# The small products of the inverse in a gated-delta layer, emitted in another order

## The chip, the cores and the metric

The kernel runs on one core of a Trainium2 chip. The metric is the device time of one execution in microseconds. The time before is the median of three runs.

## What is computed

A trunk of two layers over 256 tokens of 2048 channels. Each layer normalises its input, projects it with one wide matrix, feeds three mixers (a convolution module, a gated DeltaNet, a dilated attention) and projects their gated outputs back into the residual stream. A last normalisation follows.

The change touches only the DeltaNet's chunk rule, in which each chunk of each head needs the inverse of a unit lower triangular matrix:

```python
kk = jnp.einsum("bhncd,bhnmd->bhncm", k, k)
lower = jnp.where(strict, beta[..., :, None] * kk * decay, 0.0)
T = lax.linalg.triangular_solve(eye + lower, jnp.broadcast_to(eye, lower.shape),
                                left_side=True, lower=True, unit_diagonal=True)
w_v = jnp.einsum("bhncm,bhnmd->bhncd", T, v * beta[..., None])
```

## The kernel before

All weights stream from HBM in chunks of two (at the output projection of the last piece four) 128-row blocks: `load_weights` (L406) brings a chunk into one of four `raw` buffers, ScalarE rounds it to the high part `whi` (L182), VectorE subtracts to get the low part `wlo` (L190), and TensorE runs three products per block (L450), high by high, high by low and low by high, into an `acc` accumulator. There are three buffers for each part. This projection is a stream of matmuls that goes through the whole kernel, job after job in the order of the list `jobs`; everything else on TensorE (transposes at L230, small products at L223 through the helper `mms`) is put between two units of it.

The order on each engine is fixed when the program is built. Each piece of work is a generator that yields operations with an engine and an estimated cost; `Plan.run` takes, again and again, the operation that can start earliest by its own clocks (ties by priority), emits it, and adds its cost to that engine's clock. What one `mms(...)` call holds is one operation of the plan: nothing of another task comes between its products. Its cost is the sum of 4 times the columns over 2.4 per product, at least 53 ns.

The DeltaNet works on two chunks of 128 tokens and six heads, so on twelve 128x128 triangular matrices per layer. `inverse()` (L841 on) inverts them all. Four 32x32 diagonal blocks of each are inverted on VectorE by substitution, 48 blocks side by side, with the blocks carried there and back through DRAM. Then the inverse is put together by products on TensorE. For one pair of 32-row blocks (a, b), X = L[a,b]' T (into `psx`, copied to `Xs`), and the off-diagonal block is minus a product of X with the other diagonal inverse (into `psy`, negated into `PTs`); the first pair's block is needed transposed as well, in `T64`, which takes one further product. Both pairs done, the same step is made at 64 rows, for the six matrices of each chunk in turn (`i` is 0 or 1). In all 60 products of 32x32 and 24 of 64x64 per layer, all in float32, each of which is two matmul instructions with two weight loads.

A product of 32 rows uses a 32x32 part of TensorE's array. Which part follows from its operands: the row part from the SBUF partitions of the inputs (`Lh(hc)[a, b]` lies on partitions `a`, `Xs[b]` on `b`), the column part from the PSUM partitions of the output (`psx[b]`, `psy[a]`, `psy[b]`). This part is called the product's place here. Before the change all products of one `mms` call have the same place.

`psx` and `psy` are two of four PSUM tiles of the pool `MIX`, which transposes and all small products share. The attention's `att_pair` uses two of the pool and alternates, within one `mms` call, products of the two heads of a pair, whose operands lie in rows 0 to 63 and 64 to 127 of the array. `state(i)` waits for the inverse (`gd["inv"]`) and is the first that reads it.

Of the kernel before, what the change touches and what calls it, by code (L numbers as in the profile page):

```python
# [15 lines left out]
ALU = mybir.AluOpType  # L16
# [7 lines left out]
H = 6  # L24
# [5 lines left out]
HC = 2 * H  # L30
# [127 lines left out]
def _free(ap):  # L158
    n = 1
    for s in ap.shape[1:]:  # L160
        n *= s
    return n
# [3 lines left out]
def hybrid_trunk(ctx, tc, x, norm_w, w_in, conv_qkv_w, a_log, dt_bias, gdn_norm_w, conf_dw_w,  # L166
# [22 lines left out]
    def tt(out_, a, b, op):  # L189
        return ("dve", 70 + _free(out_) / 0.96, lambda: nc.vector.tensor_tensor(out_, a, b, op=op))  # L190

    def ts(out_, a, s1, s2, op0, op1=None):
        extra = 60 if not isinstance(s1, (int, float)) else 0

        def emit():
            if op1 is None:
                nc.vector.tensor_scalar(out_, a, s1, None, op0=op0)
            else:
                nc.vector.tensor_scalar(out_, a, s1, s2, op0=op0, op1=op1)
        return ("dve", 70 + _free(out_) / 0.96 + extra, emit)  # L200

    def cpy(out_, in_):
        return ("dve", 70 + _free(out_) / 0.96, lambda: nc.vector.tensor_copy(out_, in_))
# [14 lines left out]
    def mms(*jobs):  # L218

        def emit():  # L220
            for o, a, b, *f in jobs:
                f = f or (True, True)
                nc.tensor.matmul(o, a, b, start=f[0], stop=f[1])  # L223
        cost = sum(max(53.0, 4 * max(_free(j[1]), _free(j[2])) / 2.4) for j in jobs)
        return ("pe", cost, emit)
# [38 lines left out]
    PTs = cp.tile([128, HC, 128], F32, name="PTs")  # L264
    T64 = cp.tile([64, HC, 64], F32, name="T64")
# [285 lines left out]
    def layer(l):  # L551
# [168 lines left out]
        def decay(b):  # L720
# [28 lines left out]
            if gd["nL"] == 4:  # L749
                plan.spawn(inverse(), 11)  # L750
# [90 lines left out]
        def inverse():  # L841

            yield ("set", gd["L"])
            L = [gd["L0"], gd["L1"]]
            dr = dp.tile([HC, 4, 32, 32], F32, name="dr", tag="dr", bufs=2)
            dr2 = dp.tile([HC, 4, 32, 32], F32, name="dr2", tag="dr2", bufs=2)
            b1, b2 = yield ("get", INV, 2)
            N48, P48 = (b[:48].rearrange("p (r c) -> p r c", c=32) for b in (b1, b2))
            b3 = yield ("get", S256)

            def hop(jobs):
                def emit():
                    for o, i_ in jobs:
                        nc.gpsimd.dma_start(o, i_)
                return ("pool", 2500.0 + 1050.0 * len(jobs), emit)
            qs = [slice(b * 32, (b + 1) * 32) for b in range(4)]
            yield hop([(dr[t * H:(t + 1) * H, b].rearrange("h r c -> r h c"), L[t][qs[b], :, qs[b]])
                       for t in range(2) for b in range(4)])
            yield hop([(N48, dr.rearrange("h b r c -> (h b) r c"))])
            nc.gpsimd.memset(P48, 0.0)  # L860
            nc.gpsimd.memset(b2[:48, 0:1024:33], 1.0)
            yield ("pool", 1500.0, lambda: None)
            for j in range(31, 0, -1):
                w = 32 - j
                tmp = b3[:48, :j * w].rearrange("p (r c) -> p r c", c=w)
                yield tt(tmp, N48[:, :j, j:j + 1].to_broadcast([48, j, w]),
                         P48[:, j:j + 1, j:].to_broadcast([48, j, w]), ALU.mult)
                yield tt(P48[:, :j, j:], P48[:, :j, j:], tmp, ALU.subtract)
            yield hop([(dr2.rearrange("h b r c -> (h b) r c"), P48)])
            yield ("put", INV, [b2])  # L870
            yield ("put", S256, [b3])
            Pd, Td = yield ("get", S384, 2)
            yield hop([(PTs[qs[b], :, qs[b]], dr2[:, b].rearrange("h r c -> r h c")) for b in range(4)]
                      + [(Pd[qs[b]].rearrange("p (h c) -> p h c", c=32), dr2[:, b].rearrange("h r c -> r h c"))
                         for b in range(4)])
            yield ("dve", 500.0, lambda: nc.vector.transpose(Td, Pd))
            P3, T3 = (b.rearrange("p (h c) -> p h c", c=32) for b in (Pd, Td))
            for b in range(2):
                yield cpy(T64[qs[b], :, qs[b]], T3[qs[b]])
            Xs = b1[:, :768].rearrange("p (h c) -> p h c", c=64)  # L880

            def h3(ap, c):
                return ap.rearrange("p (h c) -> p h c", c=c)

            def Lh(hc):
                return L[hc // H][:, hc % H]
            psx, psy = yield ("get", MIX, 2)
            prs = [(slice(0, 32), slice(32, 64)), (slice(64, 96), slice(96, 128))]
            for p, (a, b) in enumerate(prs):
                yield mms(*((psx[b, hc * 32:hc * 32 + 32], Lh(hc)[a, b], T3[a, hc, :]) for hc in range(HC)))  # L890
                yield cpy(Xs[b, :, :32], h3(psx[b, :HC * 32], 32))
                yield mms(*((psy[a, hc * 32:hc * 32 + 32], Xs[b, hc, :32], P3[b, hc, :]) for hc in range(HC)))
                if p == 0:
                    yield mms(*((psy[b, hc * 32:hc * 32 + 32], P3[b, hc, :], Xs[b, hc, :32]) for hc in range(HC)))
                    yield ts(T64[b, :, a], h3(psy[b, :HC * 32], 32), -1.0, None, ALU.mult)
                yield ts(PTs[a, :, b], h3(psy[a, :HC * 32], 32), -1.0, None, ALU.mult)
            yield ("put", S384, [Pd, Td])
            a, b = slice(0, 64), slice(64, 128)
            for i in range(2):
                hs = slice(i * H, (i + 1) * H)  # L900
                yield mms(*((psx[b, j * 64:j * 64 + 64], Lh(i * H + j)[a, b], T64[:, i * H + j, :])
                            for j in range(H)))
                yield cpy(Xs[b, hs, :], h3(psx[b, :H * 64], 64))
                yield mms(*((psy[a, j * 64:j * 64 + 64], Xs[b, i * H + j, :], PTs[b, i * H + j, b])
                            for j in range(H)))
                yield ts(PTs[a, hs, b], h3(psy[a, :H * 64], 64), -1.0, None, ALU.mult)
            yield ("put", MIX, [psx, psy])
            yield ("put", INV, [b1])
            yield ("set", gd["inv"])
# [360 lines left out]
```

## Time and profile before

| | |
|---|---|
| median of 3 runs | 1005.6 us (1005.53 to 1006.33) |
| the profiled execution | 1005.26 us |
| its span | 1003.6 us |
| instructions in it | 18681 |
| ScalarE busy | 548.7 us (55%) |
| GpSimd busy | 48.2 us (5%) |
| DMA, mean over the span | 176 GB/s |

The span goes from the first instruction to the last; the profiled execution's own time has 1.7 us around it. PE is TensorE's matmuls, PEld its weight loads, DVE is VectorE, ACT ScalarE, POOL GpSimd. The end of a matmul in the profile is modelled, and matmuls overlap in time, so the duration of a row that merges several is from the first start to the last end. L223 is the line in `mms`, so all small products of the kernel stand under it, and are told apart by their shapes and tile names. `mix<-b,inv` is a product into a tile of the pool `MIX` from a tile named `b` and one named `inv` (`Xs` lies in an `inv` buffer).

### The profile page before, as it was taken

To read this page: it belongs to the slowest core of one execution; us is meant where nothing else is said; L and a number is where in the kernel's file an instruction comes from. 1 tells how busy PE (TensorE), PEld (TensorE's weight loads), DVE (VectorE), ACT (ScalarE), POOL (GpSimd) and SP (SyncE) were. 2 spreads that over 40 slices of the span, in tenths; PEclk is the share of its full clock that TensorE was granted. 3 is DMA by queue.
4 is the path that set the end of the run, shared out by engine and by line. 5 is a ranking of instruction groups with operands and counts; after the bars stand their busy time and mean duration, and the time that the engine had idled before them with its cause. 6 is when DMAs were issued, how large, how long until landed. Compare 5 with 4: busy or idle time off the path is not lost.

```text
span 1003.6 us, 18681 instructions
## 1 busy us (share of the span) xinstructions
PE 990.7 (99%) x7107; PEld 939.6 (94%) x7107; DVE 747.9 (75%) x1491; ACT 548.7 (55%) x1063; POOL 48.2 (5%) x69
## 2 busy tenths in 40 slices
PE   8999999999999999999999999999999999999996
PEld 8999999999999989888899999999999999998886
DVE  6587599998899666655557767999888987666554
ACT  7665345544676674444455633554447777544443
POOL 1000200100010000000000020002000100000000
PEclk9999999999999999999999999999999999999999
DMA  8665566654444635766656655566444456467644
GB/s 272 178 202 170 154 178 179 186 152 133 145 145 144 198 105 171 232 226 218 210 183 180 197 166 170 176 180 190 139 140 133 143 173 201 129 195 221 212 166 158
DMA packets 113365, 176.86 MB, mean 176 GB/s; under 512 B 8314, under 2 KB 80828, under 8 KB 113276
## 3 DMA queue, kind: packets, MB, share of 16 engines
q1 hardware_dynamic: 111660, 172.66, 55.9%
q0 software_dynamic: 1616, 3.02, 1.1%
q8 instruction: 55, 0.90, 0.4%
q14 instruction: 34, 0.28, 0.1%
HBM read 170.67 MB, written 4.98 MB: 175 GB/s over the span
## 4 chain that ended last, share of the span: by engine, by line
PE 96%; DMA 1%; issue 1%; ACT 1%; DVE 0%; SPq 0%; POOLq 0%; POOL 0%; ACTq 0%
PE acc L450 86%; PE mix L223 6%; PE mix L230 3%; DMA b<-in_x 1%; DMA raw<-in_w_out 1%; PE acc L459 0%; PE mix L733 0%; ACT b L182 0%; DVE wlo L190 0%; ACT whi L182 0%; SPq L406 0%; DVE HT L190 0%; ACT HT L182 0%; SPq L389 0%; PE mix L338 0%
## 5 line engine op out<-in xcount | busy, mean ns | idle before, releaser
L182 ACT ACTIVATE whi<-raw 128x768 fp32r<-128x768 f32 (+4 forms) x373 | 336.6, 902 | 390.9 <-PE acc L450 328.7
L190 DVE TENSOR_TENSOR wlo<-raw,whi 128x768 fp32r<-128x768 f32 (+4 forms) x373 | 383.1, 1027 | 204.4 <-ACT whi L182 194.9
L450 PE MATMUL acc<-HT,whi 128*128 128x256 f32 x2304 | 420.8, 283 | 0.0
L450 PEld LDWEIGHTS acc<-HT,whi 128*128 128x128 f32 x2304 | 356.1, 189 | 1.6 <-issue 1.5
L450 PE MATMUL acc<-HT,wlo 128*128 128x256 f32 x1152 | 325.4, 282 | 0.0
L450 PE MATMUL acc<-whi,HT 128*128 128x384 f32 (+1 forms) x1024 | 271.2, 346 | 0.1
L450 PEld LDWEIGHTS acc<-HT,wlo 128*128 128x128 f32 x1152 | 216.0, 188 | 0.0
L450 PEld LDWEIGHTS acc<-whi,HT 128*128 128x128 f32 x1024 | 179.6, 188 | 2.3 <-issue 1.0
L450 PE MATMUL acc<-wlo,HT 128*128 128x384 f32 (+1 forms) x512 | 172.7, 337 | 0.0
L450 PE MATMUL acc<-whi,YT 128*128 128x512 f32 (+1 forms) x512 | 152.8, 382 | 0.0
L450 PEld LDWEIGHTS acc<-whi,YT 128*128 128x128 f32 x512 | 93.9, 188 | 20.2
L187 DVE SCALAR_TENSOR_TENSOR b<-b,dw,b 128x255 f32<-128x255 f32 (+29 forms) x240 | 104.3, 461 | 0.2
L450 PE MATMUL acc<-wlo,YT 128*128 128x512 f32 (+1 forms) x256 | 97.7, 382 | 0.0
L450 PEld LDWEIGHTS acc<-wlo,HT 128*128 128x128 f32 x512 | 96.3, 188 | 0.0
L450 PEld LDWEIGHTS acc<-wlo,YT 128*128 128x128 f32 x256 | 48.2, 188 | 10.3
L230 PE MATMUL mix<-ident,b 128*128 128x128 f32 x312 | 51.1, 276 | 1.8 <-DMA b<-in_x 1.4
L182 ACT ACTIVATE b<-mix 128x256 f32<-128x256 f32 (+3 forms) x95 | 38.5, 421 | 19.0 <-PE mix L223 9.9
L187 DVE SCALAR_TENSOR_TENSOR b<-b,cw,b 128x255 f32<-128x255 f32 (+2 forms) x108 | 48.6, 473 | 0.0
L223 PE MATMUL mix<-b,b 128*128 128x128 f32 (+5 forms) x456 | 47.8, 285 | 0.4 <-ACT b L182 0.4
L223 PEld LDWEIGHTS mix<-b,b 128*128 128x128 f32 (+3 forms) x456 | 38.0, 161 | 7.5 <-issue 2.7
L230 PEld LDWEIGHTS mix<-ident,b 128*128 128x128 f32 x312 | 37.8, 141 | 7.1 <-DMA b<-in_x 2.3
L187 DVE SCALAR_TENSOR_TENSOR b<-b,b 128x256 f32<-128x256 f32 (+3 forms) x62 | 31.3, 510 | 2.7 <-ACT b L182 2.6
(149 smaller groups left out, 647.4 us busy)
## 6 DMA issues: line engine op xcount, KB each, us to landing
raw<-in_w_in SPq DMA_DIRECT2D x240, 384.0 KB, 3.1
raw<-in_w_out SPq DMA_DIRECT2D x60, 512.0 KB, 4.7
raw<-in_w_in SPq DMA_DIRECT2D x48, 512.0 KB, 3.5
raw<-in_w_in SPq DMA_DIRECT2D x15, 396.0 KB, 3.5
b<-in_x SPq DMA_DIRECT2D x12, 256.0 KB, 6.0
raw<-in_conf_pw_w SPq DMA_DIRECT2D x4, 512.0 KB, 3.2
X<-b SPq DMA_DIRECT2D x8, 256.0 KB
raw<-in_w_out SPq DMA_DIRECT2D x8, 256.0 KB
```

Of the source, the lines that this page charges most:

```text
L182: lambda: nc.scalar.activation(out_, in_, func, bias=bias, scale=scale, **kw))
L187: lambda: nc.vector.scalar_tensor_tensor(out_, a, s, b, op0=op0, op1=op1))
L190: return ("dve", 70 + _free(out_) / 0.96, lambda: nc.vector.tensor_tensor(out_, a, b, op=op))
L223: nc.tensor.matmul(o, a, b, start=f[0], stop=f[1])
L230: nc.tensor.transpose(o, a, ident)
L450: nc.tensor.matmul(o, w, m, start=first and i == 0 and not (chan and t % 2), stop=last and i == 2, skip_group_check=chan)
```

## The change

In the 32-row step the first products of both pairs are emitted in one call, alternating from pair to pair; the second products of both pairs and the product for `T64` in one call, in threes. In the 64-row step the first products of the second six matrices alternate with the second products of the first six. The copies and negations are the same, each behind the call that it needs.

```diff
             prs = [(slice(0, 32), slice(32, 64)), (slice(64, 96), slice(96, 128))]
-            for p, (a, b) in enumerate(prs):
-                yield mms(*((psx[b, hc * 32:hc * 32 + 32], Lh(hc)[a, b], T3[a, hc, :]) for hc in range(HC)))
+            yield mms(*((psx[b, hc * 32:hc * 32 + 32], Lh(hc)[a, b], T3[a, hc, :]) for hc in range(HC) for a, b in prs))
+            for a, b in prs:
                 yield cpy(Xs[b, :, :32], h3(psx[b, :HC * 32], 32))
-                yield mms(*((psy[a, hc * 32:hc * 32 + 32], Xs[b, hc, :32], P3[b, hc, :]) for hc in range(HC)))
-                if p == 0:
-                    yield mms(*((psy[b, hc * 32:hc * 32 + 32], P3[b, hc, :], Xs[b, hc, :32]) for hc in range(HC)))
-                    yield ts(T64[b, :, a], h3(psy[b, :HC * 32], 32), -1.0, None, ALU.mult)
+            (a0, b0), (a1, b1_) = prs
+
+            def third(hc):
+                c = slice(hc * 32, hc * 32 + 32)
+                return [(psy[a0, c], Xs[b0, hc, :32], P3[b0, hc, :]), (psy[a1, c], Xs[b1_, hc, :32], P3[b1_, hc, :]),
+                        (psy[b0, c], P3[b0, hc, :], Xs[b0, hc, :32])]
+            yield mms(*(m for hc in range(HC) for m in third(hc)))
+            yield ts(T64[b0, :, a0], h3(psy[b0, :HC * 32], 32), -1.0, None, ALU.mult)
+            for a, b in prs:
                 yield ts(PTs[a, :, b], h3(psy[a, :HC * 32], 32), -1.0, None, ALU.mult)
             yield ("put", S384, [Pd, Td])
             a, b = slice(0, 64), slice(64, 128)
-            for i in range(2):
-                hs = slice(i * H, (i + 1) * H)
-                yield mms(*((psx[b, j * 64:j * 64 + 64], Lh(i * H + j)[a, b], T64[:, i * H + j, :])
-                            for j in range(H)))
-                yield cpy(Xs[b, hs, :], h3(psx[b, :H * 64], 64))
-                yield mms(*((psy[a, j * 64:j * 64 + 64], Xs[b, i * H + j, :], PTs[b, i * H + j, b])
-                            for j in range(H)))
-                yield ts(PTs[a, hs, b], h3(psy[a, :H * 64], 64), -1.0, None, ALU.mult)
+
+            def down(i, j):
+                return (psx[b, j * 64:j * 64 + 64], Lh(i * H + j)[a, b], T64[:, i * H + j, :])
+
+            def up(i, j):
+                return (psy[a, j * 64:j * 64 + 64], Xs[b, i * H + j, :], PTs[b, i * H + j, b])
+            hs = [slice(i * H, (i + 1) * H) for i in range(2)]
+            yield mms(*(down(0, j) for j in range(H)))
+            yield cpy(Xs[b, hs[0], :], h3(psx[b, :H * 64], 64))
+            yield mms(*(m for j in range(H) for m in (down(1, j), up(0, j))))
+            yield cpy(Xs[b, hs[1], :], h3(psx[b, :H * 64], 64))
+            yield ts(PTs[a, hs[0], b], h3(psy[a, :H * 64], 64), -1.0, None, ALU.mult)
+            yield mms(*(up(1, j) for j in range(H)))
+            yield ts(PTs[a, hs[1], b], h3(psy[a, :H * 64], 64), -1.0, None, ALU.mult)
             yield ("put", MIX, [psx, psy])
```

## Rows read from the trace of the kernel before

**Rows 1.** Page, part 1: engine, busy us, share of the span, instructions.
```profile
PE 990.7 (99%) x7107; PEld 939.6 (94%) x7107; DVE 747.9 (75%) x1491; ACT 548.7 (55%) x1063; POOL 48.2 (5%) x69
```
**Rows 2.** Waits of TensorE: who for whom, us in total, times, longest.
```profile
PE mix L308 <- POOL pw_neg L316: 1.6, 1, 1.6
PE mix L230 <- DMA b<-in_x: 1.4, 2, 1.3
...
PE mix L230 <- DVE b L197: 0.4, 1, 0.4
```
**Rows 3.** Timeline, TensorE, layer 0: start us, us, line, operation, how many.
```profile
219.48 0.34 PE L450 MATMUL acc<-wlo,HT 128*128 128x384 f32 x1
...
220.00 0.34 PE L450 MATMUL acc<-wlo,HT 128*128 128x384 f32 x1
220.26 0.94 PE L223 MATMUL mix<-b,b 32*32 32x32 f32 x24
221.13 0.62 PE L450 MATMUL acc<-whi,HT 128*128 128x384 f32 x2
221.59 0.34 PE L450 MATMUL acc<-wlo,HT 128*128 128x384 f32 x1
```
**Rows 4.** The same timeline, a batch of 64-row products.
```profile
226.30 0.34 PE L450 MATMUL acc<-wlo,HT 128*128 128x384 f32 x1
226.57 0.91 PE L223 MATMUL mix<-T,b 64*64 64x64 f32 x12
227.41 0.62 PE L450 MATMUL acc<-whi,HT 128*128 128x384 f32 x2
227.86 0.34 PE L450 MATMUL acc<-wlo,HT 128*128 128x384 f32 x1
```
**Rows 5.** The same timeline, two batches of 32-row products back to back.
```profile
215.24 0.84 PE L223 MATMUL mix<-b,inv 32*32 32x32 f32 x21
215.90 0.21 PE L223 MATMUL mix<-inv,b 32*32 32x32 f32 x1
215.92 0.19 PE L223 MATMUL mix<-b,inv 32*32 32x32 f32 x1
...
215.96 0.19 PE L223 MATMUL mix<-b,inv 32*32 32x32 f32 x1
...
215.99 0.19 PE L223 MATMUL mix<-b,inv 32*32 32x32 f32 x1
216.01 0.82 PE L223 MATMUL mix<-inv,b 32*32 32x32 f32 x21
216.77 0.44 PE L230 MATMUL mix<-ident,b 128*128 128x128 f32 x2
```
**Rows 6.** Timeline, TensorE, layer 1: the first and last of eight batches.
```profile
706.38 0.94 PE L223 MATMUL mix<-b,b 32*32 32x32 f32 x24
...
730.90 0.91 PE L223 MATMUL mix<-PTs,inv 64*64 64x64 f32 x12
```
**Rows 7.** Timeline, start of an attention pair's first products, at three cuts.
```profile
281.02 0.38 PE L223 MATMUL mix<-b,b 64*128 64x128 f32 x2
281.02 0.19 PEld L223 LDWEIGHTS mix<-b,b 64*128 64x128 f32 x2 [0.25 <-issue]
281.02 0.30 PEld L223 LDWEIGHTS mix<-b,b 64*128 64x128 f32 x4 [0.25 <-issue]
```
**Rows 8.** Stretches: us; busy us (x) of PE, PEld, DVE, ACT, POOL; clock, DMA.
```profile
240.00:260.00 20.00, 20.00 (x133) 19.93 (x132) 17.50 (x40) 12.15 (x29) 0.00 (x0) 1.00 0.46 138
...
280.00:300.00 20.00, 20.00 (x133) 17.98 (x133) 19.29 (x61) 16.38 (x44) 4.78 (x2) 1.00 0.54 158
780.00:800.00 20.00, 20.00 (x131) 18.44 (x130) 19.55 (x62) 15.40 (x38) 4.90 (x2) 1.00 0.49 139
```
**Rows 9.** Timeline, layer 1: a low part is made, and first read.
```profile
782.40 0.95 DVE L190 TENSOR_TENSOR wlo<-raw,whi 128x768 fp32r<-128x768 f32 x1
...
785.25 0.34 PE L450 MATMUL acc<-wlo,HT 128*128 128x384 f32 x1
```

## The prediction, made before the changed kernel was built

> **What bounds the kernel now.** Page part 1 first: TensorE counts as busy for 990.7 of the span's 1003.6 us, VectorE for 747.9 [rows 1]. A busy TensorE need not be a limiting one, so next the view of its waits: it lists five, from 1.6 down to 0.4 us, 4.5 us in all, and the two above 1 us are start-up (one waits for x to arrive) [rows 2]. The reader is to see that TensorE almost never waits in the middle of the run: what it executes there, in the order written, is the time. So a microsecond of TensorE's own time saved comes off the end, provided that the other engines can follow.
>
> Then the timeline of TensorE where the inverse's small products run. They are not alone: they lie between units of the projection, whose matmuls of 384 columns follow each other every 0.17 us (three from 219.48 to 220.00, 0.52) [rows 3]. A batch of small products is an interruption of that stream, and I price it as the time by which it delays the stream: start of the last wide matmul before to start of the third after it, less 0.52.
>
> 12 products of 32 rows, which are 24 matmuls (each float32 product is two): 220.00 to 221.59 is 1.59, so the price is 1.07 [rows 3]. The 24 have 0.94 us from the first start to the last end; one lasts 0.19, so their 23 steps take 0.75, 0.0325 each. The rest, 1.07 - 0.75 = 0.32, is going into small shapes and out again, paid per interruption.
>
> 6 products of 64 rows, 12 matmuls: 226.30 to 227.86, price 1.04 [rows 4]; 0.91 less some 0.22 for one is 0.69 for the steps.
>
> The 24 products emitted as two batches back to back, 48 matmuls: 1.53 us from 215.24 to the next operation at 216.77 [rows 5]; its steps are 1.53 - 0.12 = 1.41 (the 0.12 is the step out, as 221.13 stands 0.12 behind the last small start in rows 3), with the 0.32 the price is 1.73.
>
> One layer has three of the first kind, one of the third, four of the second: 3 x 1.07 + 1.73 + 4 x 1.04 = 9.10 us. Layer 1 repeats them: eight interruptions of the same counts, the first and the last of them stand in [rows 6].
>
> **The change part by part.**
>
> No product, copy or DMA is added or lost: 60 products of 32 rows and 24 of 64 per layer (168 matmuls), and nine copies or negations on VectorE, before and after. What changes is order, and eight interruptions become five: 48 matmuls (both pairs' first products, alternating), 72 (second products of both pairs, with those for T64), then 12, 24 (`down` of the second half alternating with `up` of the first) and 12 of 64 rows.
>
> Whether neighbours at different places of the array run side by side decides everything, and the trace shows it twice. In rows 5 the first batch writes PSUM partitions 0 to 31, the second 32 to 63. Where they meet, starts of the second (from 215.90) mix with the last of the first (215.92, 215.96, 215.99): seven starts from 215.90 to 216.01 (two are left out there), 0.018 apart, against 0.0325 within a batch, so each place keeps its own pace beside the other. In the attention the two heads of a pair alternate between row halves of the array as the new order would: two 64x128 weight loads end after 0.19 us together, which is what one takes, two matmuls after 0.38, and four loads after 0.30, one step of 0.11 for two [rows 7]. So I take: each place at its own pace, the batch as long as its longest place, plus 0.01 per further place. The other end is no overlap, 0.0325 per matmul.
>
> The batch of 48 has two places: 24 steps as in rows 3, 1.07 + 0.01 = 1.08. Other end: 1.73.
>
> The batch of 72 has three places, 24 matmuls each; two of the places are exactly those of rows 5. 1.07 + 0.02 = 1.09. Three at once no row shows; bounds from the rows: 0.018 per start gives 72 x 0.018 + 0.32 = 1.62; the third place wholly behind the others 1.07 + 0.75 = 1.82; no overlap 2.66. I take 1.09, nearest to what rows 5 and 6 show of two.
>
> Of the 64-row batches two interruptions of 12 stay, 2 x 1.04; the 24 alternate between two places that share neither rows nor columns: 1.04 + 0.01 = 1.05; the other end is 1.04 + 0.69 = 1.73.
>
> The new sum is 1.08 + 1.09 + 2.08 + 1.05 = 5.30. Saved are 3.80 per layer, 7.6 us over two.
>
> Cost at nothing: the VectorE steps between batches have stream units around them before and after; no batch is needed at once. The inverse ends about two interruptions and their spacing sooner (from 220.26 to 226.57, with one batch between, they are 3.15 us apart [rows 3, 4]), so the state steps behind it can be planned some 6 us earlier. The planner's price of a batch is the sum of its products, unchanged in total, so its clock agrees with the old one outside the inverse, but it will place other work differently behind. Luck there can give back only waits in mid-run, under 1 us [rows 2]; what it can cost is the second rival.
>
> Who is late next: TensorE, 3.8 us earlier after each inverse, meets VectorE, which prepares the weights' low parts. VectorE is busy 17.5 of 20 us behind the inverse, but 19.3 and 19.6 of 20 from 280 and 780 on [rows 8]. The tightest place of mid-run: a low part is ready at 782.40 + 0.95 = 783.35 and first read at 785.25, a lead of 1.9 us [rows 9]. I expect the lead to be the same afterwards: it is set by a fixed number of weight buffers, and free time like the 2.5 us from 240 to 260 [rows 8] lets VectorE catch up 3.8 us in the 40 us before the tight stretch.
>
> A rule speaks against it. The Trainium skill says (TensorE: Matmul & The Clock Gate, section "Wait — 56ns, not 53.3ns?") that starts of matmuls never come closer than about 25 ns however small they are. By it the batches of 48 and 72 would be 1.52 and 2.12, and 4.7 us would be saved instead of 7.6. Rows 5 disagree over seven starts, 0.018 apart; whether that pace holds for 72 no row shows.
>
> **Sum.** The profiled execution took 1005.26 us: 1003.6 of span and 1.7 around it. 1005.26 - 7.6 = 997.7. The median of the runs lies 0.3 above the profiled one, so 998.0.
>
> **The rivals.**
> First, products that leave by one PSUM tile take turns. The batch of 48 sends both row places into psx, the 72 into psy. In rows 5 both series come from the same rows of the array; in rows 7 each half has a PSUM tile of its own. So no row shows two row places writing one tile. If they take turns, the 48 costs 1.73 and the 72 as well (T64's products beside one pair's, the other pair's behind), the 24 keeps its gain: 6.6 per layer, 5.0 saved, 1000.6. The Trainium skill has this as a rule (TensorEngine Tiling (Array Packing), section "Gotcha 1: PSUM Pressure": different row tiles can't access one PSUM bank at the same time). Against: the partitions written differ, as they did in rows 5. Chance 0.14, a pace of starts in the 72 slower than the 0.018 of rows 5 included.
>
> Second, VectorE becomes the bound in the tight stretches. If it does not catch up, TensorE reaches 785 3.8 us early and its lead of 1.9 is gone: it waits 1.9 us, and about as much in layer 0, whose stretch is as full. Left: 7.6 - 3.8 = 3.8, 1001.8. For it 19.3 and 19.6 of 20; against it the free time before. Chance 0.12.
>
> Third, it does not do what it says: the places don't overlap in an alternating batch, and only three interruptions fewer per layer count: 3 x 0.32 = 0.96, less the 0.1 that rows 5 already overlap, 1.7 in all, 1003.9. Against it: rows 7. Chance 0.08.
>
> Fourth, slower: a change of place costs as a change of shape does. Going from the stream into a batch takes 0.26 (220.00 to 220.26) instead of 0.17 [rows 3], 0.09 more. If the two matmuls of a product stay together, the three mixed batches change place 23, 35 and 11 times, 69 a layer: 6.2 us, less the third rival's 0.86, is 5.3 a layer, 10.7 in all, 1016. It decides from 0.012 per change on, where it eats that gain. Against: rows 7 change place at every product and show no such gap. Chance 0.04.
>
> **How the numbers follow.** The forecast has 0.62, its own range 996.5 to 999.6 (the third place wholly behind is 0.73 per layer; luck in the order gives 1 us). The first two rivals end at 1000.6 and 1001.8, so 996.4 to 1001.8 leaves out the other two and a little. About 0.2%, 2.0 us, can be told from no change: the forecast and the first two rivals are faster by more, 0.88, of which I leave 0.02 to a planned order behind the inverse that loses all of it and more: 0.86. Within: the third rival, 0.08. Slower: the fourth and that 0.02, 0.06.
>
> **What would show it.** Right: five interruptions per inverse; the batch of 48 no longer than 0.96 us and that of 72 no longer than 0.98 from first start to last end; starts in the 48 about 0.016 apart, with both places in turn; the mid-run waits of TensorE as before. First rival: the 48 at 1.6 us, the 24 of 64 rows still at 0.92. Second: TensorE waits on wlo near 780 to 790. Third: 0.0325 per matmul everywhere; fourth: more. The forecast is wrong if the batch of 72 is above 1.7 us, or if TensorE's mid-run waits grow by more than 2 us.

## The result, and the profile after

The changed kernel takes 998.4 us (median of 4 runs, 996.6 to 999.5) against 1006.0 for the kernel before (4 runs, 1005.5 to 1007.8): a ratio of 0.992, with a 95% interval of 0.990 to 0.994. The forecast was 998.0. The profiled execution took 996.6 us, with a span of 994.8.

The page's first part (engine, busy us, share of the span, instructions), to be held against [rows 1]:

```profile
PE 982.5 (99%) x7107; PEld 933.6 (94%) x7107; DVE 747.4 (75%) x1494; ACT 548.0 (55%) x1060; POOL 48.0 (5%) x69
```

TensorE has the same 7107 matmuls and is busy for 8.2 us less; the span is 8.7 us shorter (1003.55 to 994.83). So the time went where it was looked for, out of TensorE's own stream. What TensorE waits for (who for whom, us in total, times, longest), to be held against [rows 2]:

```profile
PE mix L308 <- POOL pw_neg L316: 1.6, 1, 1.6
PE mix L230 <- DMA b<-in_x: 1.3, 2, 0.9
PE mix L223 <- DVE PTs L197: 0.6, 1, 0.6
PE acc L459 <- DVE HT L190: 0.4, 1, 0.4
PE mix L223 <- DVE inv L203: 0.2, 1, 0.2
```

The two lines with L223 are new: small products of the inverse now wait for a copy and a negation on VectorE. They are small, and the forecast did not have them.

Now the inverse of layer 0 on TensorE's timeline (start us, us, line, operation, how many). The 48 matmuls in place of two batches like that of [rows 3]:

```profile
211.35 0.34 PE L450 MATMUL acc<-wlo,HT 128*128 128x384 f32 x1
211.62 0.95 PE L223 MATMUL mix<-b,b 32*32 32x32 f32 x48
212.49 0.62 PE L450 MATMUL acc<-whi,HT 128*128 128x384 f32 x2
212.95 0.34 PE L450 MATMUL acc<-wlo,HT 128*128 128x384 f32 x1
```

They last 0.95 us, and the 24 alone lasted 0.94. From the last wide matmul before to the third after it is 212.95 - 211.35 = 1.60, less the 0.52 of the stream: a price of 1.08.

The start and end of the 72, to be held against [rows 5]:

```profile
215.82 0.22 PE L223 MATMUL mix<-b,inv 32*32 32x32 f32 x2
215.83 0.21 PE L223 MATMUL mix<-inv,b 32*32 32x32 f32 x1
215.87 0.20 PE L223 MATMUL mix<-b,inv 32*32 32x32 f32 x2
215.88 0.19 PE L223 MATMUL mix<-inv,b 32*32 32x32 f32 x1
...
216.58 0.19 PE L223 MATMUL mix<-inv,b 32*32 32x32 f32 x1
216.70 0.44 PE L230 MATMUL mix<-ident,b 128*128 128x128 f32 x2
```

From 215.82 to 216.58 is 0.76 us for 71 steps, 0.0107 each. T64's matmuls, `mix<-inv,b`, begin at 215.88 as the second and at 216.58 as the 24th, 22 steps of 0.032: each place keeps about the 0.0325 of [rows 3], and three run beside each other.

The 24 of 64 rows, beginning and end, to be held against [rows 4]:

```profile
223.05 0.34 PE L450 MATMUL acc<-wlo,HT 128*128 128x384 f32 x1
223.32 0.27 PE L223 MATMUL mix<-T,b 64*64 64x64 f32 x1
223.32 0.27 PE L223 MATMUL mix<-PTs,inv 64*64 64x64 f32 x1
...
224.01 0.22 PE L223 MATMUL mix<-PTs,inv 64*64 64x64 f32 x1
224.16 0.62 PE L450 MATMUL acc<-whi,HT 128*128 128x384 f32 x2
224.62 0.34 PE L450 MATMUL acc<-wlo,HT 128*128 128x384 f32 x1
```

Both places start at 223.32 and end together; the price is 224.62 - 223.05 - 0.52 = 1.05.

**Where the time came from.** Both kernels run the same 5856 matmuls of the projection stream (L450) in the same order, so one can count them from the start and compare the time at which the same matmul begins. In the table, the layer stretches begin and end at such matmuls (numbers 1380, 2300, 4300 and 5500 of L450) and hold the inverse and the attention behind it; "between" holds the rest between numbers 120 and the last.

| us | start to no. 120 | layer 0 | layer 1 | between | last L450 to the end |
|---|---|---|---|---|---|
| before | 31.95 | 188.34 | 225.17 | 537.10 | 20.99 |
| after | 31.49 | 183.25 | 222.29 | 537.09 | 20.70 |
| difference | -0.46 | -5.09 | -2.88 | -0.01 | -0.29 |

Expected were -3.80 in each layer. Start and end differ from one execution to the next; in a second profile of the changed kernel (first experiment) they are 32.19 and 21.42, while the three columns between agree to 0.01 us. So the layers can be read to about 0.1 us, and 0.75 us of this profile's 8.7 is start and end.

Layer 0 can be cut once more, at number 1993. Up to there, with the inverse, both kernels have the same matmuls, and the changed one takes 136.52 us instead of 140.32: 3.80 less, the forecast itself. From 1993 to 2300, the end of the attention, where the edit changes nothing, it takes 46.73 instead of 48.02: the other 1.29.

In layer 1, TensorE's timeline around the last two batches (in brackets the idle time ahead, and for whom):

```profile
711.89 0.34 PE L450 MATMUL acc<-wlo,HT 128*128 128x384 f32 x1
712.48 0.27 PE L223 MATMUL mix<-T,b 64*64 64x64 f32 x1 [0.25 <-DVE inv L203]
...
715.44 0.34 PE L450 MATMUL acc<-wlo,HT 128*128 128x384 f32 x1
716.33 0.91 PE L223 MATMUL mix<-PTs,inv 64*64 64x64 f32 x12 [0.55 <-DVE PTs L197]
```

A batch otherwise starts 0.27 after the last wide matmul (211.35 to 211.62). Here it is 0.59 and 0.89: 0.32 and 0.62 late. VectorE's timeline says why:

```profile
710.88 0.95 DVE L190 TENSOR_TENSOR wlo<-raw,whi 128x768 fp32r<-128x768 f32 x1
711.87 0.56 DVE L203 COPY inv<-mix 64x384 f32<-64x384 f32 x1
...
714.62 0.56 DVE L203 COPY inv<-mix 64x384 f32<-64x384 f32 x1
715.21 0.48 DVE L187 SCALAR_TENSOR_TENSOR b<-b,dw,b 128x250 f32<-128x250 f32 x1
715.72 0.55 DVE L197 TENSOR_SCALAR PTs<-mix 64x384 f32<-64x384 f32 x1
```

The copy that the 24 need ends at 712.43, behind a low part of the weights that VectorE took first; the negation that the last 12 wait for, as they write the part of `psy` that it reads, ends at 716.27, behind a copy and another step (L187). From 714.62 on VectorE goes from one instruction to the next; the inverse's next batch is due sooner than its queue gets to it. In layer 0, instead, 1.29 us more than 3.80 came back. The kernel before waits twice at the end of that layer's attention:

```profile
367.90 1.28 PE L230 MATMUL mix<-ident,b 128*128 128x128 f32 x7
369.55 0.70 PE L230 MATMUL mix<-ident,b 128*128 128x128 f32 x3 [0.36 <-DVE b L197]
370.69 0.65 PE L223 MATMUL mix<-b,b 128*64 128x256 f32 x2 [0.44 <-ACT b L182]
```

Both waits are gone in the changed kernel (no such line stands in its list above). They cost more than the 0.80 us that the brackets show, which count only from a matmul's modelled end: these ten transposes and eight products take 3.96 us here, until the stream goes on at 371.86, and in the changed kernel ten transposes in a row take 1.07 (from 354.57) and eight such products 0.80 (from 372.34). So 2.1 us were lost; the changed order pays some of it back with seven interruptions in this stretch instead of four. It has 84 matmuls of the stream just ahead of the last transposes, where the kernel before has 48. That is the planned order behind the inverse, which came out differently.

VectorE in the full stretches (columns as in [rows 8]), and a low part just ahead of the second of them (columns as in [rows 9]):

```profile
280.00:300.00 20.00, 20.00 (x131) 18.27 (x130) 19.47 (x63) 16.55 (x42) 2.45 (x2) 1.00 0.47 140
780.00:800.00 20.00, 20.00 (x134) 17.87 (x133) 19.15 (x56) 13.38 (x31) 2.35 (x1) 1.00 0.47 139
```

```profile
769.67 0.95 DVE L190 TENSOR_TENSOR wlo<-raw,whi 128x768 fp32r<-128x768 f32 x1
...
772.77 0.34 PE L450 MATMUL acc<-wlo,HT 128*128 128x384 f32 x1
```

The low part is ready at 770.62 and read at 772.77, a lead of 2.15 us; the next has 2.10, the least near there. The least in mid-run is 1.97 (read at 334.95, in layer 0), where it was 1.9.

### The profile page after: what moved, and what is told of

Read it like the earlier page. It is cut to its first block, busy times and chain, and to the rows that moved or that the text cites. A ratio compares the mean times of both kernels' runs of the same rounds, so it can differ in the third digit from the quotient of the medians.

```text
span 994.8 us, 18677 instructions
## 1 busy us (share of the span) xinstructions
PE 982.5 (99%) x7107; PEld 933.6 (94%) x7107; DVE 747.4 (75%) x1494; ACT 548.0 (55%) x1060; POOL 48.0 (5%) x69
## 4 chain that ended last, share of the span: by engine, by line
PE 96%; DMA 1%; DVE 1%; issue 1%; ACT 0%; SPq 0%; POOLq 0%; POOL 0%; ACTq 0%
PE acc L450 86%; PE mix L223 6%; PE mix L230 4%; DMA raw<-in_w_out 1%; DMA b<-in_x 1%; PE acc L459 0%; PE mix L733 0%; DVE wlo L190 0%; DVE b L187 0%; SPq L406 0%; DVE HT L190 0%; DVE inv L203 0%; ACT HT L182 0%; SPq L389 0%; PE mix L338 0%
## 5 line engine op out<-in xcount | busy, mean ns | idle before, releaser
L182 ACT ACTIVATE whi<-raw 128x768 fp32r<-128x768 f32 (+4 forms) x373 | 336.6, 902 | 382.0 <-PE acc L450 340.3
L450 PE MATMUL acc<-HT,whi 128*128 128x256 f32 x2304 | 421.0, 283 | 0.0
L450 PEld LDWEIGHTS acc<-HT,whi 128*128 128x128 f32 x2304 | 356.5, 189 | 1.6 <-issue 1.5
L450 PE MATMUL acc<-HT,wlo 128*128 128x256 f32 x1152 | 325.5, 283 | 0.0
L450 PE MATMUL acc<-whi,HT 128*128 128x384 f32 (+1 forms) x1024 | 271.0, 346 | 0.0
L450 PEld LDWEIGHTS acc<-HT,wlo 128*128 128x128 f32 x1152 | 215.9, 187 | 0.0
L450 PEld LDWEIGHTS acc<-whi,HT 128*128 128x128 f32 x1024 | 179.5, 189 | 1.8 <-issue 1.2
L450 PE MATMUL acc<-wlo,HT 128*128 128x384 f32 (+1 forms) x512 | 172.7, 337 | 0.0
L450 PE MATMUL acc<-whi,YT 128*128 128x512 f32 (+1 forms) x512 | 152.8, 382 | 0.0
L450 PEld LDWEIGHTS acc<-whi,YT 128*128 128x128 f32 x512 | 93.9, 188 | 20.2
L187 DVE SCALAR_TENSOR_TENSOR b<-b,dw,b 128x255 f32<-128x255 f32 (+29 forms) x240 | 105.1, 461 | 0.3
L450 PE MATMUL acc<-wlo,YT 128*128 128x512 f32 (+1 forms) x256 | 97.7, 382 | 0.0
L450 PEld LDWEIGHTS acc<-wlo,HT 128*128 128x128 f32 x512 | 96.3, 188 | 0.0
L450 PEld LDWEIGHTS acc<-wlo,YT 128*128 128x128 f32 x256 | 48.2, 188 | 10.3
L182 ACT ACTIVATE b<-mix 128x384 f32<-128x384 f32 (+3 forms) x96 | 39.4, 425 | 19.6 <-PE mix L223 12.7
L187 DVE SCALAR_TENSOR_TENSOR b<-b,cw,b 128x255 f32<-128x255 f32 (+2 forms) x108 | 48.6, 473 | 0.0
L223 PE MATMUL mix<-b,b 128*128 128x128 f32 (+5 forms) x456 | 46.0, 286 | 0.0
L223 PEld LDWEIGHTS mix<-b,b 128*128 128x128 f32 (+3 forms) x456 | 36.3, 161 | 6.7 <-issue 2.2
L187 DVE SCALAR_TENSOR_TENSOR b<-b,b 128x256 f32<-128x256 f32 (+3 forms) x62 | 31.3, 510 | 1.7 <-ACT b L182 1.6
```

The costliest lines, as they stand in the source:

```text
L182: lambda: nc.scalar.activation(out_, in_, func, bias=bias, scale=scale, **kw))
L187: lambda: nc.vector.scalar_tensor_tensor(out_, a, s, b, op0=op0, op1=op1))
L450: nc.tensor.matmul(o, w, m, start=first and i == 0 and not (chan and t % 2), stop=last and i == 2, skip_group_check=chan)
```

## The experiments

Every kernel was timed beside the kernel before on the same chip, and the ratio is to that; the two with one run have none. Sizes of batches are steps, first start to last start.

**The changed kernel again**, unedited.

> The changed kernel once more. Theory (each place of the array runs at its own pace): the batches of 48, 72 and 24 matmuls have again 0.95, 0.95 and 0.92 us from first start to last end (0.76, 0.76 and 0.70 of steps), the time is 997 to 999.5 us, 0.8% under the kernel before. Of the 8.7 us between the two profiles 7.6 are the batches; the other 1.1 comes from waits (start-up, the end of layer 0's attention, the end of the kernel) less the 0.9 us of new waits in layer 1, and should vary from run to run. Rival (the order that the planner makes behind the inverse gives the gain): the batches matter less than these waits, and the sum of the waits moves by several us between profiles.

997.7 us (6 runs), ratio 0.992 (0.990 to 0.994). The batches take 0.756, 0.762, 0.690, 0.697 and 0.690; layers 183.25 and 222.29. The result repeats, and so do the waits in layer 1; what differs between the two profiles is start and end.

**The same batches, not alternating.** Same calls, same copies, same order of everything else; only the order of the products within the three mixed batches is by place.

```diff
-  ... for hc in range(HC) for a, b in prs))
+  ... for a, b in prs for hc in range(HC)))
-  yield mms(*(m for hc in range(HC) for m in third(hc)))
+  yield mms(*(third(hc)[p] for p in range(3) for hc in range(HC)))
-  yield mms(*(m for j in range(H) for m in (down(1, j), up(0, j))))
+  yield mms(*(down(1, j) for j in range(H)), *(up(0, j) for j in range(H)))
```

> The same five batches, the same order on every engine, but within a batch the products stand place after place instead of alternating. Theory: the 48 takes 1.41 us of steps, as the two batches back to back did before, the 72 about 2.1, the 24 of 64 rows about 1.3; 2.6 us more per layer, 5.2 in all: 1003.5 us, 0.25% under the kernel before. Rival (the gain comes from fewer interruptions and another planned order): as fast as the changed kernel, 998.4. Rival (one PSUM tile is written by one row place at a time): the seams show no mixing, otherwise as the theory.

1002.0 us (6 runs), ratio 0.996 (0.995 to 0.998), where the expectation was 1003.5. The batches take 1.409, 2.070 and 1.211, in sum 2.475 more per layer; layer 0 is 185.78, 2.53 longer than the changed kernel's. Layer 1 is 223.76, only 1.47 longer: the longer batches leave VectorE the time it lacked, and no wait for its copies is left. TensorE's timeline where the 72 pass from T64's neighbours to T64's own products:

```profile
217.71 1.51 PE L223 MATMUL mix<-b,inv 32*32 32x32 f32 x45
219.03 0.21 PE L223 MATMUL mix<-inv,b 32*32 32x32 f32 x1
...
219.14 0.82 PE L223 MATMUL mix<-inv,b 32*32 32x32 f32 x21
```

Only at the seam, over a few matmuls, do the places run beside each other, as in [rows 5]. So it is the alternation that makes them overlap, and it is worth about 2.5 of the 3.8 us per layer; the rest are three interruptions fewer and the seams.

**One half of the change alone**: the 32-row part with the 64-row loop of before, and the reverse.

```diff
 # only32: 32-row step of the changed kernel, then
+            for i in range(2):
+                ...   # down, copy, up, negation as before
 # only64: 32-row step of the kernel before, then down/up of the changed kernel
```

> Only the 32-row part changed, the 64-row part as before. Theory: 3 x 1.07 + 1.73 - 1.08 - 1.09 = 2.77 us per layer, 5.5 in all: 1000.4 us, 0.55% under the kernel before. Rival (planned order): this and the run with only the 64-row part changed don't add up to the whole change, by more than 2 us.

> Only the 64-row part changed, the 32-row part as before. Theory: 4 x 1.04 - 3.13 = 1.03 us per layer, 2.1 in all: 1003.9 us, 0.2% under the kernel before. Rival (planned order): anything within 2 us of the kernel before, and not the difference that is missing in the run with only the 32-row part.

Only 32 rows: 999.5 us (6 runs), ratio 0.994 (0.992 to 0.995), layers -4.02 and -2.43 against before. Only 64 rows: 1002.5 (7 runs), ratio 0.997 (0.996 to 0.998), layers -2.27 and -0.96. The prices give 2.77 and 1.03 per layer (4.94 less 2.17 and 4.16 less 3.13). So in layer 0 both carry the same surplus of some 1.25 us, and it can't be a batch's: either half alone takes away the two waits at the end of the attention, and from number 1993 on both take the 46.73 of the changed kernel. In layer 1 the half with 64 rows gives its 1.03 almost whole (0.96) and the half with 32 rows loses 0.34 to a wait. The second wait of layer 1, 0.62 us, comes only with both halves.

**A fourth place.** The batch of 72 gets a product of `P3[b1_]` and `Xs[b1_]` as well, at the one place still free: 96 matmuls.

```diff
-                        (psy[b0, c], P3[b0, hc, :], Xs[b0, hc, :32])]
+                        (psy[b0, c], P3[b0, hc, :], Xs[b0, hc, :32]), (psy[b1_, c], P3[b1_, hc, :], Xs[b1_, hc, :32])]
 ...   # and the planner's price of the batch stays that of three places
```

> The batch of 72 gets a fourth place: 24 further matmuls per layer whose result goes to PSUM partitions 96 to 127 and is read by nothing; the planner's price is left as it was. Theory (each place at its own pace): 96 matmuls in 0.77 us of steps, where 72 had 0.763; the work is free and the time stays at 997.7. Rival (the 72 is already at the pace at which products can be issued, 0.0107 us per start): 96 x 0.0107 = 1.02 us of steps, 0.26 more per layer.

997.9 us in one run, which tells nothing finer than about 1 us (ten runs of the changed kernel lie from 996.6 to 1001.9); the trace does. The 96 take 0.830, layer 0 is 183.32 and layer 1 222.30, 0.07 and 0.01 longer. The end of the batch on TensorE's timeline:

```profile
217.65 0.21 PE L223 MATMUL mix<-b,inv 32*32 32x32 f32 x2
217.67 0.19 PE L223 MATMUL mix<-inv,b 32*32 32x32 f32 x1
217.68 0.19 PE L223 MATMUL mix<-b,inv 32*32 32x32 f32 x1
217.69 0.21 PE L223 MATMUL mix<-inv,b 32*32 32x32 f32 x2
```

Here two places start almost at once and the two others 0.015 us later, a round of four in 0.033, 0.008 per start: 24 matmuls at a fourth place cost 0.07 us, where 24 alone cost 0.75. The theory said 0.77. The 0.06 more arise from the middle of the batch on: there the starts, about evenly spaced until then with 0.032 a round, slip and go on in pairs. These runs don't explain it.

**Alternating in threes.** Three products of one place, then three of the next.

```diff
-  ... for hc in range(HC) for a, b in prs))
+  ... for q in range(0, HC, 3) for a, b in prs for hc in range(q, q + 3)))
```

and likewise in the two other mixed batches.

> The three mixed batches alternate in blocks of three products of a place (six matmuls) instead of one; everything else is as in the changed kernel. In the unmixed run one seam between two places saved 0.12 us of 32-row products (1.53 - 1.41, 2.31 - 2.07) and 0.18 of 64-row ones (1.39 - 1.21). Theory of a short look-ahead, that is of a seam's saving for each of 7, 11 and 3 seams: 1.53 - 0.84 = 0.76 (the floor of one place) to 0.85 us for the 48, 2.31 - 1.32 = 0.99 for the 72, 1.39 - 0.54 = 0.85 for the 24. Rival (a look-ahead over whole blocks of six): 0.76, 0.76 and 0.70 as with single products. Rival (only direct neighbours overlap): 1.4, 2.0 and 1.3.

998.2 us in one run. The batches take 0.839, 1.169 and 0.860, that is 0.08, 0.41 and 0.16 more, and layer 0 is 0.67 longer (183.92). For the 48 and the 24 that is what the theory said, for the 72 it is 0.18 more. TensorE's timeline of the 72, start and end:

```profile
216.28 0.37 PE L223 MATMUL mix<-b,inv 32*32 32x32 f32 x9
...
217.39 0.25 PE L223 MATMUL mix<-inv,b 32*32 32x32 f32 x3
217.57 0.44 PE L230 MATMUL mix<-ident,b 128*128 128x128 f32 x2
```

Its 71 steps of 0.0165 on the mean are about half of the 0.0325 of one place: two places run beside each other while the third waits, and at the end (217.39) three matmuls of one place run alone. TensorE goes past matmuls that wait for their place, but not far: with six matmuls in a row at a place, two places overlap nearly in full, and three do not. Layer 1 stays at 222.29: there the longer batches only eat what the waits for VectorE had cost (0.3 us of them is left instead of 0.8).

**The copies on whichever engine is free.** The nine copies and negations of the inverse may go to ScalarE or VectorE, as the planner finds.

```diff
-                yield cpy(Xs[b, :, :32], h3(psx[b, :HC * 32], 32))
+                yield copy(Xs[b, :, :32], h3(psx[b, :HC * 32], 32))
-            yield ts(T64[b0, :, a0], h3(psy[b0, :HC * 32], 32), -1.0, None, ALU.mult)
+            yield copy(T64[b0, :, a0], h3(psy[b0, :HC * 32], 32), -1.0)
```

and the other six in the same way.

> The changed kernel, with the nine copies and negations of the step open to ScalarE or VectorE, as the planner chooses. Theory: the two new waits in layer 1 (TensorE 0.32 and 0.65 us late for a copy and a negation that stand behind conv taps in VectorE's queue) come from VectorE's order and go: 1.0 us less than the changed kernel, 996.7. Rival (planned order): another wait of about 1 us turns up elsewhere; no difference.

995.8 us (5 runs), ratio 0.990 (0.989 to 0.992); layers 182.55 and 221.36. Layer 1 is 0.93 shorter than the changed kernel's, about the 0.94 of the two waits, and TensorE no longer waits for a copy of the inverse. ScalarE's timeline, with the two copies of the 64-row step, of which the first was late and the second held up the negation:

```profile
707.95 0.49 ACT L182 ACTIVATE inv<-mix 64x384 f32<-64x384 f32 x1 [0.98 <-PE mix L223]
709.97 0.49 ACT L182 ACTIVATE inv<-mix 64x384 f32<-64x384 f32 x1 [0.17 <-PE mix L223]
```

ScalarE had been idle for 0.98 and 0.17 us when the matmuls let them start. So the lost microsecond was the place of these steps in VectorE's queue. Not VectorE as such: the planned order differs too, and in the last experiment the waits vanish while the steps stay on VectorE. Layer 0 gains 0.70, which had no such waits; up to number 1993 it is the changed kernel's to 0.01 us, and the gain is all at the end of the attention, so again planned order.

**The 64-row level in two batches instead of three**: all 12 `down`, then all 12 `up`, each alternating between its two halves, with the second half's results in the other partitions of `psx` and the first half's in those of `psy` so that the two places, which share rows, share no columns.

```diff
-            yield mms(*(down(0, j) for j in range(H)))
-            ...
+            yield mms(*(down(i, j) for j in range(H) for i in range(2)))
+            for i in range(2):
+                yield cpy(Xs[b, hs[i], :], h3(psx[out[0][i], :H * 64], 64))
+            yield mms(*(up(i, j) for j in range(H) for i in range(2)))
+            for i in range(2):
+                yield ts(PTs[a, hs[i], b], h3(psy[out[1][i], :H * 64], 64), -1.0, None, ALU.mult)
```

> The 64-row level in two interruptions instead of three: the first products of both sets of six alternate, one set writing PSUM partitions 64 to 127 and the other 0 to 63 (its copy moves it to partitions 64 to 127), then the second products of both sets likewise. Theory: 2 x 1.05 instead of 1.04 + 1.05 + 1.04, 1.03 us less per layer, 2.1 in all, and both sets' copies lie between the same two batches: 995.6 us, 1.0% under the kernel before, if the waits in layer 1 stay as they are. Rival (VectorE in layer 1): two copies in a row before the second batch make it wait 0.5 us longer per layer, 996.6. Rival: places that share their input rows (both sets of first products come from rows 0 to 63) do not overlap at 64 rows, the steps are 1.39 instead of 0.70: no gain, 998.4.

997.3 us (5 runs), ratio 0.991 (0.990 to 0.992); layers 183.78 and 220.97. The first batch of 24 takes 0.697 as expected, the second 1.005 in layer 0 and 1.452 in layer 1, because both copies now lie between the two batches. TensorE's and VectorE's timelines in layer 1:

```profile
714.88 0.33 PE L223 MATMUL mix<-PTs,inv 64*64 64x64 f32 x2
715.64 0.91 PE L223 MATMUL mix<-PTs,inv 64*64 64x64 f32 x22 [0.44 <-DVE inv L203]
```

```profile
713.93 0.56 DVE L203 COPY inv<-mix 64x384 f32<-64x384 f32 x1
714.52 0.48 DVE L187 SCALAR_TENSOR_TENSOR b<-b,dw,b 128x250 f32<-128x250 f32 x1
715.03 0.55 DVE L203 COPY inv<-mix 64x384 f32<-64x384 f32 x1
```

Two matmuls ran, and the third waited for the second copy, which ended at 715.58. Layer 0 is 0.76 shorter than the changed kernel's up to number 1993, the 1.03 less the 0.31 by which the second batch is late, to 0.04 us. From there on it takes 48.03, as in the kernel before: the list of TensorE's waits has again the two lines for `b` from L197 and from L182, 0.4 us each. So the planned order ate the gain.

**Both together**: two batches at 64 rows and the copies on either engine.

> The two 64-row interruptions of the run before, with the copies and negations open to either engine. Theory: four batches of 0.76, 0.76, 0.70 and 0.70 us of steps and no wait inside the second 64-row batch (the run before lost 0.31 and 0.76 us there, for a copy behind conv taps in VectorE's queue): 1.03 us less per layer than with the copies open alone, 2.1 in all, 993.7 us, 1.2% under the kernel before. Rival (planned order): the wait of 1.1 us at the end of layer 0's attention, which the kernel before and the run before have and the others don't, is there again: 994.8.

994.6 us (4 runs), ratio 0.989 (0.988 to 0.990): the lowest median, with the shortest layers, 181.50 and 220.18. The interval overlaps that of the open copies alone; the layers tell the two apart. TensorE's timeline in layer 1:

```profile
706.87 0.92 PE L223 MATMUL mix<-T,b 64*64 64x64 f32 x24
...
709.99 0.92 PE L223 MATMUL mix<-PTs,inv 64*64 64x64 f32 x24
```

Both batches are whole, with 0.697 each. Against the kernel with open copies alone the layers are 1.05 and 1.18 shorter; by the prices one interruption less is worth 1.03.

**The batches priced as they run.** The planner's price of a batch is the sum of its products, which is two or three times what an alternating batch takes. Here each mixed batch gets a half, a third or a half of it, by its number of places, first in the changed kernel, then in the one with both together, which the second expectation names as the first run.

```diff
-            yield mms(*(m for hc in range(HC) for m in third(hc)))
+            op = mms(*(m for hc in range(HC) for m in third(hc)))
+            yield (op[0], op[1] / 3, op[2])
 ...   # the other mixed batches likewise, with / 2
```

> The changed kernel, with the planner's price of the three mixed batches divided by their number of places (2, 3, 2), as they run. Theory: the two new waits in layer 1 come from a batch that the planner thinks longer than it is, so that it puts too little of the stream behind it before the next; they go or halve: 996.9 to 997.3 us. Rival (they come from VectorE's queue alone, as the run with the copies open to either engine says): they stay at 0.9 us, 997.7.

> The first run of this call, with the four mixed batches priced at one place's share as well. Theory: the batches are the same and nothing waits for them, so the time is that of the first run within 0.5 us. Rival (planned order): it differs by 1 us or more, by waits at the end of layer 0's attention.

Both came out slower than the same kernel with the old price: 1000.0 us (5 runs), ratio 0.995 (0.993 to 0.996), and 997.9 (5 runs), ratio 0.992 (0.991 to 0.993). In layer 1 the first theory held: the two waits for the copy and the negation are gone, with both still on VectorE. The copy comes up sooner in VectorE's queue, and ahead of the last batch stand 18 matmuls of the stream instead of 12; the layer takes 220.89 instead of 222.29. The second kernel has 220.18 as before. In layer 0 the true price costs 3.72 and 3.48 us (186.97 and 184.98), of which TensorE's timeline at the end of the attention shows 2.1 in one wait (here the second kernel; the first has the same wait in its list):

```profile
363.62 0.60 PE L230 MATMUL mix<-ident,b 128*128 128x128 f32 x4
366.33 1.05 PE L230 MATMUL mix<-ident,b 128*128 128x128 f32 x5 [2.11 <-DVE b L197]
```

It is the place of the two waits of the kernel before. The same ten transposes and eight products that take 1.87 us undisturbed take 5.24 here, from 363.62 to 368.86, and 6.31 in the first kernel, so nearly all of the loss lies in this one place. What goes with it in all thirteen profiles is the length of the stream ahead of the last transposes: 24 matmuls in these two kernels, 48 in the two that wait less (the kernel before and the one with two batches at 64 rows), 72 or 84 in those that don't wait. Why the planner puts so few there in some orders was not settled.

## Why the prediction was right

**The terms.** The forecast priced the batches at 1.08, 1.09, 2 x 1.04 and 1.05; the trace of after gives 1.08, 0.76 of steps with the same way in and out (1.08), 1.04 and 1.05. Where layer 0 can be read apart from what comes behind, up to number 1993, the sum comes out at the forecast 3.80. The mechanism is the one named: each place keeps its own pace beside the others, close to the 0.0325 per matmul of [rows 3], and three interruptions fewer do the rest; the kernel that does not alternate loses 2.5 us per layer of it. The sentence on the third place names rows 5 and 6, but it is rows 5 and 7 that show two places; the value taken there, that a third place adds nothing, is the one the trace confirmed.

**The rule that spoke against it.** In the changed kernel the starts of the 72 stand 0.0107 us apart on the mean, and those of the 96 with a fourth place 0.0087. The Trainium skill's figure of about 25 ns between starts (TensorE: Matmul & The Clock Gate, section "Wait — 56ns, not 53.3ns?") does not hold here, and the measurement decides. Within one place it could not show, as that pace is slower, 0.0325.

**The first rival** wanted the 48 at 1.6 us. They take 0.95, with both row places writing one PSUM tile at the same columns, on other partitions. The Trainium skill's rule that row tiles can't use one PSUM bank at once (TensorEngine Tiling (Array Packing), section "Gotcha 1: PSUM Pressure") did not show in these batches. **The third and fourth** fall with the same rows; what the third would have looked like is the kernel that does not alternate, 1002.0 us. **The second** wanted waits for low parts near 785; there are none, and the least lead is 1.97 us, as expected.

**What was off.** Two terms that were set at about nothing were not. "VectorE steps between batches have stream units around them" failed in layer 1: a copy and a negation came 0.32 and 0.62 us late, and the 24 behind the first of these waits took 0.07 more steps (0.766). The step looked at units before and after a batch and not at what stands in VectorE's queue ahead of the copy; the time between two batches had shrunk, the queue had not. Two kernels without these waits, one with the steps on either engine and one with another planned order, agree with that; neither changes the queue alone.

And luck in the planned order was bounded by 1 us "under", from the waits in mid-run; it gave 1.29 in layer 0. The bound was too low because the list of waits shows 0.80 us where 2.1 were lost. As the orders with true prices show, luck can also cost 3.5, and for that the likeliest case's own range had no room. The two errors, 1.29 more in layer 0 and 0.92 less in layer 1, cancelled to 0.37 us, so 7.97 us between start and end met a forecast of 7.6. The batches were forecast rightly; that the total fits so closely is luck.

## What to carry to other kernels

Small matmuls at different places of the array, with output partitions of their own, cost TensorE little beyond the longest place, up to four places, if they alternate product by product; estimate such a batch by its longest place plus the 0.32 us of leaving and entering the wide stream. Four places are shown for products of 32 rows, two for 64. When a chain of batches and copies shrinks, look at the queue of the engine that copies; letting the copies go to whichever engine is idle helped here. A wait in the list counts from a modelled end and can cost more than it shows: compare the same work with and without it. An order planned with prices is not a neutral part of a change: it moved single layers by 1.3 us one way and 3.7 the other here, so compare stretches with the same work, cut right behind the edit, before putting a difference down to it.

## What the runs showed of the hardware that had not been expected

- Four places of 32 by 32 overlap almost fully: 96 matmuls in 0.830 us of steps, 24 at one place in 0.750.
- Places that share rows overlap as well as places that share neither rows nor columns: 24 of 64 rows take 0.697 us in both cases (the two-batch level with open copies, and the changed kernel), where 12 take 0.690. In the attention two places of 64 rows and all 128 columns run side by side [rows 7], each with a PSUM tile of its own. Of 32x32 or 64x64 places that share columns no run has a batch.
- Matmuls of another place begin before earlier ones of the first have begun, but only over a short distance: 48 in blocks of 24 take 1.409 us of steps, in blocks of six 0.839, in twos (one product at a time) 0.756.
